# Two pairs of experts gathered at once from two fp32r parts, and each pair's second product behind the next pair's first ones

## The chip, the cores and the metric

The kernel runs on one core of one Trainium2 chip. The metric is the device time of one execution in microseconds (us); lower is better. The kernel before took 1582.65 us (median of 3 runs, 1581.34 to 1585.59). Engines are named as the profile names them: PE is TensorE's matmuls and PEld its weight loads, DVE is VectorE, ACT ScalarE, POOL GpSimd, SP SyncE, which issues most of the transfers from HBM.

## The reference

The program computes a two-layer first block over 256 tokens of 1024 features and then a two-layer second block. The change is in the first block alone, whose layers end with a mixture of experts:

```python
for i in range(DEPTH):                    # DEPTH = 2
    ...                                   # a token mixer and an attention over 256 memory tokens give o
    x = layer_norm(ALPHA * x + o, ln1_g[i], ln1_b[i])
    f = grouped_moe(x, router_w, router_b, w_gate[i], w_up[i], w_down[i])
    x = layer_norm(ALPHA * x + f, ln2_g[i], ln2_b[i])

def grouped_moe(x, ...):                  # 16 experts; each token goes to two of one group of four
    ...
    for e in range(N_EXPERTS):
        h = silu(xt @ w_gate[e]) * (xt @ w_up[e])        # 1024 -> 512
        out = out + combine[:, e:e + 1] * (h @ w_down[e])  # 512 -> 1024
```

All is fp32. `combine` is zero except for a token's two experts. setup_inputs draws the weights at random.

## The kernel before, in words

**Data.** The 256 tokens stand in two tiles of 128 (`TT = 2`), and the 1024 features in eight blocks of 128 (`KD = 8`). fp32 matmuls run in several passes of the array, so the larger products are written as sums of products of fp32r parts: `split` (L461 to L463) makes a high part with one ScalarE copy (L462) and the low part with one VectorE subtraction (L463). The expert products are fp32r too; the gather's are fp32.

**Experts.** An expert takes up to 64 tokens (`CAP = 64`), and the experts run in eight pairs, so that a pair fills the 128 positions of a tile: expert `ea` the first 64, `eb` the other 64. For a token that has the expert, `slot` holds its position there. Per pair `moe` (L1061 to L1193) does this:
- *gather* (L1076 to L1106): VectorE compares `slot` with a row of numbers (L1082), which gives a one-hot matrix `d` (tokens by positions); TensorE multiplies the standardised tokens `t` with it, sixteen fp32 matmuls of 128 columns (L1089), and `affine` evacuates the result with the norm's gain and bias into `xe` (features by positions). Then TensorE turns `d` (L1096) and fetches the combine weights of the positions (L1099).
- *up*: for two halves `j` of the features and for gate and up (`m`), four steps of 128 features, at each one matmul of `ea` (64 positions, 512 columns) and one of `eb` (L1139). The two write the two halves of one PSUM bank and use different columns of the array.
- ScalarE and VectorE compute the activation `eg` (L1148 to L1150).
- *scatter* of the pair before (L1113), then the gather of the next pair.
- four transposes of `eg` (L1159), evacuated by a ScalarE copy (L1160).
- *down*: for two halves of the output eight steps of 512 columns, `ea` and `eb` beside each other (L1169). ScalarE and VectorE evacuate each half in two fp32r parts, scaled by the combine weights (L1172, L1173); the next pair's scatter adds them to the tokens.

The first pair's gather is traced with a higher priority (offset 600), and its second half after the first half of pair 0's up matmuls. `scaled_rows` (L641) adds the tokens' own share in pair 0, with four row products on TensorE (L598). Behind the last scatter `keep_warm` (L592) issues matmuls whose results nobody uses.

**Before the experts.** `out_norm` (L884 to L923) ends the mixer with the product by `w_out`, then computes the moments, the router's chain of small VectorE operations (L942 to L1002), and the standardised tokens `t` (`standard`, L632). In layer 0 it also computes the other layer's memory products there (`mem_k`, `mem_v`); in layer 1 it issues 14 `keep_warm` matmuls.

**Loads.** Weights come in loads of 1 MiB, issued on SyncE's queue (L373) in a fixed order: gate, up and down are two loads each, so six for an expert and 96 for a layer. `Stream` puts a load into a slot of its own (eight) or, up to the number given by `limit`, into a slot lent from the first block's own `ESLOTS = 13`, which the mixer and `out_norm` use for their tensors. A slot becomes free when the matmuls that read it are done, and then the next load is issued. `out_norm` sets the limit to `ESLOTS - 5` in layer 0 and `ESLOTS - 2` in layer 1 and then to one more; `moe` to `ESLOTS - 2` and `ESLOTS - 1`, and from pair 6 on lower.

**Order.** A planner writes each engine's queue before the run. It takes what is ready by its own model of costs, by priority in the order in which the code traces the operations (`high_priority` moves them ahead). Matmuls that write the same PSUM bank stay in the order in which they are traced. On the chip an engine executes its queue in that fixed order, whatever is ready.

Of the kernel before, what the change touches and what calls it, by code (L numbers as in the profile page):

```python
# [17 lines left out]
P = 128  # L18
S = 256
TT = 2  # L20
D = 1024
KD = 8
NE = 16
CAP = 64
# [17 lines left out]
Q_UV = "gpsimd"  # L42
WARM0, WARM1, WARM2 = 12, 14, 22
E_X1 = "vector"
ESLOTS = 13
GCOL = 12
S0 = 0.0
S1 = 0.0
# [363 lines left out]
class Net:  # L412
# [240 lines left out]
    def first_block(self):  # L653
        nc, I, tc = self.nc, self.I, self.tc
        with ExitStack() as ctx:
# [15 lines left out]
            n = len(ROWS1)  # L671
# [44 lines left out]
            for i in range(2):  # L716
                if i:
                    xh, xl = sl.get([P, KD, S], F32R, "xh"), sl.get([P, KD, S], F32R, "xl")
                    tmp = sl.get([P, 4, 512], name="tmp")
                    self.scratch = itertools.cycle([tmp[:, k] for k in range(4)]).__next__  # L720
                    self.split_feat(t, KD, xh, xl, bias=self.ln_cols(0, "ln2"))
                    sl.put(tmp)
                parts = self.mixer(i, xh, xl, memT, t)
                route, t = self.out_norm(i, parts)
                t = self.moe(i, route, t)
                if self.stop in (f"x1_{i}", f"comb_{i}", f"x2_{i}"):
                    if self.stop == f"x2_{i}" and i:
                        self.scaled_rows(1, "ln2", t, self.xres, 1.0)
                        self.dumpit("x2_1", self.xres)
                    return None  # L730
# [60 lines left out]
    def mixer(self, i, xh, xl, memT, t2):  # L791
# [9 lines left out]
        if i == 0:  # L801
# [23 lines left out]
            chunk(0, lambda b, ps: nc.scalar.activation(uT[:, b], ps, AF.Gelu))  # L825
            sl.put(xh, xl)
            tok = sl.get([P, 2, 4, S], F32R, "tok")
            t = self.small([P, 512], "eg", bufs=1).rearrange("p (h t d) -> p h t d", h=2, t=TT)
            for hp in range(2):
                mix = self.psum("a").rearrange("p (h t d) -> p h t d", h=2, t=TT)  # L830
                for h in range(2):
# [54 lines left out]
    def out_norm(self, i, parts):  # L886


        nc, sl = self.nc, self.sl
        v = nc.vector  # L890
        x = self.xres
        st = [self.small([P, 2, 6], f"ln_st{tt}", bufs=1) for tt in range(TT)]
        raw = [self.psum("a")[:, :NE] for _ in range(TT)]
        self.stream.limit(ESLOTS - (2 if i else 5))
        for half in range(2):
            ps = [self.psum() for _ in range(TT)]
            run(self.gemm_stream(None, None, [("wout", i, half, j) for j in (1, 0)], ps,
                                 parts=[(p[:, 0], p[:, 1]) for p in parts]))
# [12 lines left out]
        sl.put(*parts)  # L911
        t = sl.get([P, TT, D], name="t")
        self.stream.limit(ESLOTS - (1 if i else 4))
        self.mom = self.moments(st, "ln")
        if i:
            self.keep_warm(WARM1, self.C("ident"), yT[:, 3])
        route = self.router(i, raw, self.mom)
        self.standard(x, t, self.mom)
        if i == 0:
            self.mem_k(1, "gpsimd")  # L920
            self.mem_v(1, "gpsimd")
            sl.put(self.mh, self.ml)
        return route, t  # L923

    def beats(self, s, name):

# [131 lines left out]
                for tt in range(TT):  # L1058
                    v.bn_stats(st[tt][:, half], f[:, tt, half * 512:half * 512 + 512])

    def moe(self, i, route, t):  # L1061


        nc, sl = self.nc, self.sl
# [1 line left out]
        comb, slot = route  # L1066
        f = self.xres
        self.dumpit(f"comb_{i}", comb)
        xe = self.small([P, KD, P], "xe", bufs=1)
        self.stream.limit(ESLOTS - (1 if i else 2))  # L1070
        iota = self.C("iota")
        cols = self.ln_cols(i, "ln1")

        def gather(pr):


            ea = 2 * pr
            d, sct = [x[:, 0].rearrange("p (t s) -> p t s", t=TT) for x in self.hl_pair(1, TT * P)]
            d = d.bitcast(F32).rearrange("p t (e c) -> p t e c", e=2)
            es = slice(ea, ea + 2)  # L1080
            for tt in range(TT):
                v.tensor_tensor(d[:, tt], iota[:, None, :].to_broadcast([P, 2, CAP]),  # L1082
                                slot[:, tt, es, None].to_broadcast([P, 2, CAP]), op=ALU.is_equal)
            for k4 in range(2):
                ps = self.psum("a").rearrange("p (k s) -> p k s", k=4)
                for k in range(4):
                    kk = 4 * k4 + k
                    for tt in range(TT):
                        nc.tensor.matmul(ps[:, k], t[:, tt, kk * P:kk * P + P],  # L1089
                                         d[:, tt].rearrange("p e c -> p (e c)"), start=tt == 0, stop=tt == TT - 1)  # L1090
                self.affine(xe[:, 4 * k4:4 * k4 + 4], ps, cols, 4 * k4, "va"[k4])
                if k4 == 0:
                    yield
            st = self.psum("a")
            for tt in range(TT):
                nc.tensor.transpose(st[:, tt * P:tt * P + P], d[:, tt].rearrange("p e c -> p (e c)"),  # L1096
                                    self.C("ident"))
            for tt in range(TT):
                nc.tensor.matmul(st[:, TT * P:TT * P + 2], d[:, tt].rearrange("p e c -> p (e c)"), comb[:, tt, es],  # L1099
                                 start=tt == 0, stop=tt == TT - 1)  # L1100
            v.tensor_copy(sct, st[:, :TT * P].rearrange("p (t s) -> p t s", t=TT))
            wt = self.small([P, 1], "slotw")
            for e in range(2):
                cs = slice(e * CAP, e * CAP + CAP)
                v.tensor_copy(wt[cs], st[cs, TT * P + e:TT * P + e + 1])
            yield sct, wt  # L1106

        def scatter(sct, y, half):
            hs = slice(half * 512, half * 512 + 512)
# [4 lines left out]
            for tt in range(TT):  # L1114
                v.tensor_tensor(f[:, tt, hs], f[:, tt, hs], ps[tt], op=ALU.add)

        last = None
        with self.tc.high_priority(offset=600):
            first = gather(0)
            next(first)  # L1120
        for pr in range(NE // 2):
            if pr == 6:
                self.stream.limit(0 if i else ESLOTS - 6)
                self.stream.keep = i
            ea, eb = 2 * pr, 2 * pr + 1
            if pr:
                sct, wt = nxt
            gu = [self.psum() for _ in range(2)]
            for j in range(2):
                if pr == 0 and j:  # L1130
                    sct, wt = next(first)
                for m in range(2):
                    w = [self.stream.get(("moe", i, e, 2 * m + j)).rearrange("p (k n) -> p k n", n=512)
                         for e in (ea, eb)]
                    for k in range(4):
                        kk = 4 * j + k
                        for e in range(2):
                            es = slice(e * CAP, e * CAP + CAP)
                            nc.tensor.matmul(gu[m][es], xe[:, kk, es], w[e][:, k], start=kk == 0,  # L1139
                                             stop=kk == KD - 1)  # L1140
                    for e in (ea, eb):
                        self.stream.done(("moe", i, e, 2 * m + j))
# [1 line left out]
                self.scaled_rows(i, "ln1", t, f, ALPHA)  # L1144
                self.dumpit(f"x1_{i}", f)
            g, u = gu
            eg = self.small([P, 512], "eg", bufs=1)
            nc.scalar.activation(eg, g, AF.Tanh, scale=0.5)  # L1148
            v.scalar_tensor_tensor(eg, eg, 1.0, g, op0=ALU.add, op1=ALU.mult)  # L1149
            v.scalar_tensor_tensor(eg, eg, 0.5, u, op0=ALU.mult, op1=ALU.mult)  # L1150
            if last is not None:
                for half in range(2):
                    scatter(last[0], last[1][half], half)
            if pr + 1 < NE // 2:
                *_, nxt = gather(pr + 1)
            hT = eg.rearrange("p (k s) -> p k s", k=4)
            pt = self.psum("a").rearrange("p (k s) -> p k s", k=4)
            for k in range(4):
                nc.tensor.transpose(pt[:, k], eg[:, k * P:k * P + P], self.C("ident"))  # L1159
            nc.scalar.copy(hT, pt)  # L1160
            last = sct, [self.hl_pair(1, 512) for _ in range(2)]
            for half in range(2):
                yh, yl = [x[:, 0] for x in last[1][half]]
                yp = self.psum()
                w = [self.stream.get(("moe", i, e, 4 + half)).rearrange("p (k n) -> p k n", n=512) for e in (ea, eb)]
                for k in range(4):
# [4 lines left out]
                    self.stream.done(("moe", i, e, 4 + half))  # L1171
                nc.scalar.activation(yh, yp, AF.Identity, scale=wt)  # L1172
                v.scalar_tensor_tensor(yl, yp, wt, yh.bitcast(F32), op0=ALU.mult, op1=ALU.subtract)  # L1173
        st = [self.small([P, 2, 6], f"ln_st{tt}", bufs=1) for tt in range(TT)]
        for half in range(2):
            scatter(last[0], last[1][half], half)
# [5 lines left out]
        else:  # L1182
            self.presplit([("w", 0, "fq", 0, "2")], lambda w, k: w[:, k:k + 1], 4)
        self.overflow(i, t, comb, slot, f, st)
        sl.put(t)
        self.mom = self.moments(st, "ln")
        if i:
            t = self.slots.get([P, TT, D], name="t2")
# [1088 lines left out]
```

## Time and profile before

| | |
|---|---|
| median of 3 runs | 1582.65 us |
| the profiled execution | 1589.67 us |
| its span, first to last instruction | 1588.0 us |
| mean granted TensorE clock | 0.98 |
| PE busy | 1489.8 us, 94% of the span |
| PEld busy | 1022.0 us |
| DVE busy | 897.8 us, 57% |
| ACT busy | 585.4 us, 37% |
| q1 (SyncE's transfers) | 335.61 MB |

All rows are of the one profiled execution, with times in us from the start of its span. Busy times are unions: two matmuls side by side count once. A row of a timeline groups like instructions that follow each other; its length runs from the first start to the last end, and matmuls overlap by a little over a tenth of a us, so the next row starts before the one above has ended. The granted clock is the share of full speed that the chip allowed TensorE. The expert stage of layer 0 lies from 141 to 385 us, that of layer 1 from 498 to 736 us.

### The profile page before, as it was taken

Reading aid. Unit: us, or ns where it says so; the run is one execution under the profiler, and the core shown is the slowest. Engines: PE = TensorE matmul, PEld = TensorE weight load, DVE = VectorE, ACT = ScalarE, POOL = GpSimd, SP = SyncE. Lnnn points to the kernel's source line nnn. Section 1 sums busy time; section 2 is a strip of 40 time slices with the busy share of each in tenths; the row PEclk is TensorE's granted clock in tenths of the full one; section 3 lists DMA queues with packets and bytes.
Section 4 is the critical chain, followed back from the end, with each engine's and each line's share of the span. In section 5 each row is a group of like instructions: output and inputs, shape, how many; then the busy total and the mean of one; then the engine's idle time right before and its main releaser. Section 6 shows DMA issues by size and latency. Waiting matters only on the chain.

```text
span 1588.0 us, 24343 instructions
## 1 busy us (share of the span) xinstructions
PE 1489.8 (94%) x9570; PEld 1022.0 (64%) x9570; DVE 897.8 (57%) x1906; ACT 585.4 (37%) x1196; POOL 83.2 (5%) x112
## 2 busy tenths in 40 slices
PE   9999999998999999998999889999999998899998
PEld 8885444433996445434766667777776676677776
DVE  6662323224775323224857778566766587784765
ACT  6541111111541111112645542355454565233653
POOL 0022000001000000003100010100000000010001
PEclk9999999999999999999999999999999999799999
DMA  9866999987284999964433442125454355211353
GB/s 362 342 245 244 398 421 421 421 345 319 81 316 184 395 421 421 421 252 166 139 106 118 148 146 68 55 93 186 159 201 150 113 174 179 69 64 41 117 202 133
DMA packets 56574, 350.75 MB, mean 221 GB/s; under 512 B 7434, under 2 KB 8456, under 8 KB 17030
## 3 DMA queue, kind: packets, MB, share of 16 engines
q1 hardware_dynamic: 51542, 335.61, 54.6%
q0 software_dynamic: 2112, 8.03, 1.5%
q10 hardware_dynamic: 2800, 5.49, 1.3%
q8 instruction: 77, 1.26, 0.3%
q14 instruction: 43, 0.35, 0.1%
HBM read 338.90 MB, written 3.67 MB: 216 GB/s over the span
## 4 chain that ended last, share of the span: by engine, by line
PE 39%; DVE 9%; DMA 2%; ACT 2%; issue 1%; ACTq 0%; DVEq 0%
PE ps_h L505 4%; PE ps_h L506 4%; PE ps_g L505 4%; PE ps_g L506 4%; PE ps_h L507 4%; PE ps_g L507 4%; PE ps_a L2022 3%; PE ps_b L2022 3%; PE ps_a L551 1%; DVE wl L463 1%; PE ps_a L1520 1%; DVE pad L2056 1%; PE ps_a L1543 1%; PE ps_b L551 1%; PE ps_b L1520 1%
## 5 line engine op out<-in xcount | busy, mean ns | idle before, releaser
L463 DVE TENSOR_TENSOR wl<-w_w,wh 128x512 fp32r<-128x512 f32 (+1 forms) x346 | 231.9, 685 | 116.4 <-ACT wh L462 115.3
L462 ACT ACTIVATE wh<-w_w 128x512 fp32r<-128x512 f32 (+1 forms) x354 | 215.4, 624 | 220.4 <-PE ps_g L507 90.0
L1139 PE MATMUL ps_g<-w_e,xe 128*64 128x512 f32 x616 | 184.8, 594 | 0.0
L506 PE MATMUL ps_h<-wl,hh 128*128 128x512 f32 (+2 forms) x272 | 109.3, 404 | 3.4 <-DVE wl L463 3.3
L506 PE MATMUL ps_g<-wl,hh 128*128 128x512 f32 (+2 forms) x272 | 109.0, 405 | 2.8 <-DVE wl L463 2.5
L1139 PE MATMUL ps_g<-w_x,xe 128*64 128x512 f32 x304 | 111.1, 594 | 0.0
L505 PE MATMUL ps_g<-wh,hh 128*128 128x512 f32 (+2 forms) x272 | 104.6, 409 | 4.5 <-ACT wh L462 4.1
L1139 PEld LDWEIGHTS ps_g<-w_e,xe 128*64 128x64 f32 x616 | 56.4, 137 | 80.9 <-issue 77.4
L507 PE MATMUL ps_h<-wh,hlo 128*128 128x512 f32 (+2 forms) x272 | 107.2, 396 | 0.0
L505 PE MATMUL ps_h<-wh,hh 128*128 128x512 f32 (+2 forms) x272 | 104.3, 404 | 2.9 <-ACT wh L462 2.1
L507 PE MATMUL ps_g<-wh,hlo 128*128 128x512 f32 (+2 forms) x272 | 105.7, 393 | 0.0
L1173 DVE SCALAR_TENSOR_TENSOR wl<-ps_g,slotw,wh 128x512 fp32r<-128x512 f32 x32 | 24.0, 751 | 126.6 <-ACT wh L1172 126.6
L1169 PE MATMUL ps_g<-w_e,eg 128*64 128x512 f32 x272 | 81.6, 596 | 6.8 <-ACT eg L1160 6.8
L1149 DVE SCALAR_TENSOR_TENSOR eg<-eg,ps_g 128x512 f32<-128x512 f32 x16 | 11.0, 688 | 119.7 <-ACT eg L1148 119.7
L462 ACT ACTIVATE wh<-w_x 128x512 fp32r<-128x512 f32 (+1 forms) x88 | 53.8, 623 | 57.0 <-PE ps_g L507 25.6
L1148 ACT ACTIVATE eg<-ps_g 128x512 f32<-128x512 f32 x16 | 9.6, 597 | 175.2 <-PE ps_g L1139 175.2
L583 ACT ACTIVATE xe<-ps_a,pcols 128x128 f32<-128x128 f32 x64 | 25.1, 457 | 121.2 <-PE ps_a L1089 117.0
L1089 PEld LDWEIGHTS ps_a<-wh,t_e 128*128 128x128 f32 x512 | 60.0, 192 | 12.0 <-issue 9.7
L506 PEld LDWEIGHTS ps_h<-wl,hh 128*128 128x128 f32 x272 | 51.9, 191 | 21.1 <-DVE wl L463 10.1
L1172 ACT ACTIVATE wh<-ps_g,slotw 128x512 fp32r<-128x512 f32 x32 | 22.0, 687 | 117.4 <-PE ps_g L1169 101.7
L1169 PE MATMUL ps_g<-w_x,eg 128*64 128x512 f32 x184 | 59.5, 596 | 5.7 <-ACT eg L1160 5.7
L506 PEld LDWEIGHTS ps_g<-wl,hh 128*128 128x128 f32 x272 | 52.3, 192 | 19.0 <-DVE wl L463 10.9
(783 smaller groups left out, 3212.9 us busy)
## 6 DMA issues: line engine op xcount, KB each, us to landing
w_e<-in_moe_dram SPq DMA_DIRECT2D x111, 1024.0 KB, 10.5
w_x<-in_moe_dram SPq DMA_DIRECT2D x61, 1024.0 KB, 10.6
w_w<-in_win_dram SPq DMA_DIRECT2D x56, 1024.0 KB, 4.9
w_w<-in_moe_dram SPq DMA_DIRECT2D x20, 1024.0 KB, 11.4
w_x<-in_wkv_dram SPq DMA_DIRECT2D x8, 1024.0 KB, 13.4
w_w<-in_wo_dram SPq DMA_DIRECT2D x8, 1024.0 KB, 4.9
w_x<-in_wout_dram SPq DMA_DIRECT2D x5, 1024.0 KB, 8.1
w_e<-in_winb_dram SPq DMA_DIRECT2D x5, 1024.0 KB, 9.6
```

The source lines that it names most:

```text
L462: self.nc.scalar.activation(hi, src, AF.Copy)
L463: self.q(eng).tensor_tensor(lo, src, hi.bitcast(F32), op=ALU.subtract)
L505: nc.tensor.matmul(o, xh[:, kk, ts], wh[:, k], start=f, stop=False)
L506: nc.tensor.matmul(o, xh[:, kk, ts], wl[:, k], start=False, stop=False)
L507: nc.tensor.matmul(o, xl[:, kk, ts], wh[:, k], start=False, stop=e)
L551: nc.tensor.transpose(ps[:rows, b, tt * P:tt * P + P], src[:, tt, (b0 + b) * rows:(b0 + b + 1) * rows], self.C("ident"))
L583: self.nc.scalar.activation(out[:, k], src[:, k], AF.Identity, bias=bk, scale=gk)
L1089: nc.tensor.matmul(ps[:, k], t[:, tt, kk * P:kk * P + P], d[:, tt].rearrange("p e c -> p (e c)"), start=tt == 0, stop=tt == TT - 1)
L1139: nc.tensor.matmul(gu[m][es], xe[:, kk, es], w[e][:, k], start=kk == 0, stop=kk == KD - 1)
L1169: nc.tensor.matmul(yp[es], hT[:, k, es], w[e][:, k], start=k == 0, stop=k == 3)
L1520: nc.tensor.matmul(s[:, h], qT[:, h0 + h, tt * P:tt * P + P], kT[:, h0 + h, :nk], start=True, stop=False)
L2022: ins = self.nc.tensor.matmul(out, lhsT, rhs, start=start, stop=stop)
```

## The change

- The standardised tokens `t` are split in `out_norm` into two fp32r parts, `th` and `tl`, by four ScalarE copies and four VectorE subtractions of 512 columns; they take two slots.
- `gather` serves two pairs at once: one-hot matrices of four experts (256 columns) are multiplied with both parts, four fp32r matmuls per block of features, 32 in all, and `xe` holds two pairs. Turning the one-hot matrix and fetching the weights follow for both pairs. The one-hot matrices lie in a slot of their own.
- A turn of the loop now traces: up of pair `pr`, the transposes of pair `pr - 1`, the scatter of pair `pr - 2`, in odd turns the gather of the pairs `pr + 1` and `pr + 2`, and down of pair `pr - 1`. A ninth turn has no up. The whole first gather stands ahead of up 0, at offset 600.
- `eg` has two buffers. `ESLOTS` is 12, so the limits of the loads change.

```diff
-ESLOTS = 13
+ESLOTS = 12
...
 out_norm:
-        self.stream.limit(ESLOTS - (2 if i else 5))
+        self.stream.limit(ESLOTS - (4 if i else 7))
...
         t = sl.get([P, TT, D], name="t")
-        self.stream.limit(ESLOTS - (1 if i else 4))
+        parts = [sl.get([P, TT, D], F32R, n) for n in ("th", "tl")]
...
         self.standard(x, t, self.mom)
+        for half in range(2):
+            hs = slice(half * 512, half * 512 + 512)
+            for tt in range(TT):
+                self.split(t[:, tt, hs], *(p[:, tt, hs] for p in parts))
...
 moe:
-        xe = self.small([P, KD, P], "xe", bufs=1)
-        self.stream.limit(ESLOTS - (1 if i else 2))
+        xe = self.small([P, KD, 2, P], "xe", bufs=1)
+        self.stream.limit(ESLOTS - (4 if i else 5))
...
+        oneslot = sl.get([P, 6, TT * P], F32R, "onehot")
...
 gather:
-            for k4 in range(2):
-                ps = self.psum("a").rearrange("p (k s) -> p k s", k=4)
-                for k in range(4):
-                    kk = 4 * k4 + k
-                    for tt in range(TT):
-                        nc.tensor.matmul(ps[:, k], t[:, tt, kk * P:kk * P + P],
-                                         d[:, tt].rearrange("p e c -> p (e c)"), start=tt == 0, stop=tt == TT - 1)
-                self.affine(xe[:, 4 * k4:4 * k4 + 4], ps, cols, 4 * k4, "va"[k4])
-                if k4 == 0:
-                    yield
+            for k2 in range(4):
+                ps = self.psum("a").rearrange("p (k s) -> p k s", k=2)
+                for k in range(2):
+                    kk = 2 * k2 + k
+                    for n, p in enumerate(parts):
+                        for tt in range(TT):
+                            nc.tensor.matmul(ps[:, k], p[:, tt, kk * P:kk * P + P],
+                                             d[:, tt].rearrange("p e c -> p (e c)"), start=n + tt == 0,
+                                             stop=n + tt == 2)
+                self.affine(xe[:, 2 * k2:2 * k2 + 2].rearrange("p k q s -> p k (q s)"), ps, cols, 2 * k2, "va")
...
+        for pr in range(pairs + 1):
+            if pr == 0:
+                with self.tc.high_priority(offset=600):
+                    slots[0], slots[1] = gather(0)
+            if pr == 6:
+                self.stream.limit(0 if i else ESLOTS - 7)
+                self.stream.keep = i
+            nxt = up(pr) if pr < pairs else None
+            if pr:
+                hT = turned(eg)
+                if last is not None:
+                    for half in range(2):
+                        scatter(last[0], last[1][half], half)
+                if pr % 2 and pr + 1 < pairs:
+                    slots[pr + 1], slots[pr + 2] = gather(pr + 1)
+                    if pr + 3 == pairs:
+                        sl.put(*parts)
+                sct, wt = slots.pop(pr - 1)
+                last = sct, down(pr - 1, hT, wt)
+            eg = nxt
```

`up`, `turned` and `down` hold the instructions that stood in the loop before, unchanged but for the doubled `xe`.

## Rows read from the trace of the kernel before

**Rows 1.** The page: busy share of DMA in 40 slices of 39.7 us.

```profile
DMA  9866999987284999964433442125454355211353
```

**Rows 2.** Windows: stretch, us, busy PE, PEld, DVE, ACT, POOL, clock, DMA, GB/s.

```profile
141.40:384.80 243.40, 231.96 (x1153) 102.27 (x1152) 64.83 (x135) 32.56 (x65) 0.00 (x0) 1.00 0.95 393
498.20:736.10 237.90, 227.84 (x1147) 101.42 (x1146) 65.15 (x138) 31.48 (x63) 0.00 (x0) 1.00 0.87 357
155.00:330.00 175.00, 167.46 (x861) 77.79 (x858) 49.37 (x106) 24.16 (x48) 0.00 (x0) 1.00 1.00 415
330.00:341.00 11.00, 11.00 (x58) 5.22 (x58) 2.28 (x7) 0.00 (x0) 0.00 (x0) 1.00 0.53 206
```

**Rows 3.** Timeline of TensorE, one pair of layer 0: start, length, operation [idle before].

```profile
172.23 0.59 PE L1139 MATMUL ps_g<-w_e,xe 128*64 128x512 f32 x1
...
186.06 0.73 PE L1113 MATMUL ps_a<-wh,wl 128*128 128x512 f32 x2
...
188.01 3.73 PE L1089 MATMUL ps_a<-wh,t_e 128*128 128x128 f32 x32
191.58 0.38 PE L1096 MATMUL ps_a<-consts,wh 128*128 128x128 f32 x2
...
192.17 0.63 PE L1159 MATMUL ps_a<-consts,eg 128*128 128x128 f32 x4
193.82 0.65 PE L1169 MATMUL ps_g<-w_e,eg 128*64 128x512 f32 x2 [1.02 <-ACT eg L1160]
...
200.74 0.60 PE L1139 MATMUL ps_g<-w_e,xe 128*64 128x512 f32 x2
```

**Rows 4.** Waits of TensorE, 141.4 to 384.9 us: total us, times, longest.

```profile
PE ps_g L1169 <- ACT eg L1160: 7.2, 8, 1.1
PE ps_a L1159 <- DVE eg L1150: 2.3, 3, 0.8
PE ps_a L1113 <- ACT wh L1172: 1.7, 2, 0.8
```

**Rows 5.** Groups by line, TensorE, 141.4 to 384.9 us: busy, mean ns, idle before.

```profile
L598 PE MATMUL ps_a<-rows,pick 50*128 50x512 f32 x4 | 1.5, 445 | 0.0
```

**Rows 6.** Timeline of TensorE, late pairs of layer 0.

```profile
286.19 1.46 PE L1169 MATMUL ps_g<-w_e,eg 128*64 128x512 f32 x6
287.48 1.02 PE L1139 MATMUL ps_g<-w_e,xe 128*64 128x512 f32 x2
288.43 0.74 PE L1113 MATMUL ps_a<-wh,wl 128*128 128x512 f32 x2
...
290.50 3.65 PE L1139 MATMUL ps_g<-w_e,xe 128*64 128x512 f32 x14
294.08 0.71 PE L1089 MATMUL ps_a<-wh,t_e 128*128 128x128 f32 x4
...
322.74 0.59 PE L1169 MATMUL ps_g<-w_x,eg 128*64 128x512 f32 x1
...
356.32 0.59 PE L1169 MATMUL ps_g<-w_e,eg 128*64 128x512 f32 x1
```

**Rows 7.** Timeline of SyncE's queue: the last expert loads of both layers.

```profile
341.37 0.90 SPq L373 DMA_DIRECT2D w_e<-in_moe_dram  x2
...
687.39 8.70 SPq L373 DMA_DIRECT2D w_x<-in_moe_dram  x4
```

**Rows 8.** DMA issues, 141 to 341 us: count, size, us from issue to landing.

```profile
w_e<-in_moe_dram SPq DMA_DIRECT2D x44, 1024.0 KB, 11.7
```

**Rows 9.** Timeline of TensorE in the mixer of layer 1.

```profile
404.47 0.28 PE L523 MATMUL ps_g<-xh_e,wh 128*128 128x256 f32 x1
404.59 0.28 PE L524 MATMUL ps_g<-xl_e,wh 128*128 128x256 f32 x1
```

**Rows 10.** Groups by line, weight loads, 404.7 to 413 us.

```profile
L523 PEld LDWEIGHTS ps_g<-xh_e,wh 128*128 128x128 f32 x24 | 4.6, 190 | 0.0
```

**Rows 11.** The page, costliest groups: busy, mean ns, idle before and its releaser.

```profile
L463 DVE TENSOR_TENSOR wl<-w_w,wh 128x512 fp32r<-128x512 f32 (+1 forms) x346 | 231.9, 685 | 116.4 <-ACT wh L462 115.3
```

More of the change, by code (lines that the diff above doesn't have):

```diff
@@ L723, in first_block @@
                 parts = self.mixer(i, xh, xl, memT, t)
-                route, t = self.out_norm(i, parts)
-                t = self.moe(i, route, t)
+                route, t, parts = self.out_norm(i, parts)
+                t = self.moe(i, route, t, parts)
                 if self.stop in (f"x1_{i}", f"comb_{i}", f"x2_{i}"):
@@ L827, in mixer @@
             tok = sl.get([P, 2, 4, S], F32R, "tok")
-            t = self.small([P, 512], "eg", bufs=1).rearrange("p (h t d) -> p h t d", h=2, t=TT)
+            t = self.small([P, 512], "eg", bufs=2).rearrange("p (h t d) -> p h t d", h=2, t=TT)
             for hp in range(2):
@@ L922, in out_norm @@
             sl.put(self.mh, self.ml)
-        return route, t
+        return route, t, parts
     def beats(self, s, name):
@@ L1059, in overflow, with moe @@
                     v.bn_stats(st[tt][:, half], f[:, tt, half * 512:half * 512 + 512])
-    def moe(self, i, route, t):
+    def moe(self, i, route, t, parts):
         nc, sl = self.nc, self.sl
@@ L1068, in moe @@
         self.dumpit(f"comb_{i}", comb)
-        xe = self.small([P, KD, P], "xe", bufs=1)
-        self.stream.limit(ESLOTS - (1 if i else 2))
+        xe = self.small([P, KD, 2, P], "xe", bufs=1)
+        self.stream.limit(ESLOTS - (4 if i else 5))
         iota = self.C("iota")
         cols = self.ln_cols(i, "ln1")
+        oneslot = sl.get([P, 6, TT * P], F32R, "onehot")
+        scts = [oneslot[:, n].rearrange("p (t s) -> p t s", t=TT) for n in range(4)]
+        onehot = oneslot[:, 4:].rearrange("p t (e c) -> p t e c", e=4)
@@ L1074, in gather @@
         def gather(pr):
             ea = 2 * pr
-            d, sct = [x[:, 0].rearrange("p (t s) -> p t s", t=TT) for x in self.hl_pair(1, TT * P)]
-            d = d.bitcast(F32).rearrange("p t (e c) -> p t e c", e=2)
-            es = slice(ea, ea + 2)
+            d = onehot
             for tt in range(TT):
-                v.tensor_tensor(d[:, tt], iota[:, None, :].to_broadcast([P, 2, CAP]),
-                                slot[:, tt, es, None].to_broadcast([P, 2, CAP]), op=ALU.is_equal)
@@ L1094, in gather @@
[L1094 to L1106, printed above, removed]
+                v.tensor_tensor(d[:, tt], iota[:, None, :].to_broadcast([P, 4, CAP]),
+                                slot[:, tt, ea:ea + 4, None].to_broadcast([P, 4, CAP]), op=ALU.is_equal)
+            for k2 in range(4):
[8 more added lines that the diff above has]
+                self.affine(xe[:, 2 * k2:2 * k2 + 2].rearrange("p k q s -> p k (q s)"), ps, cols, 2 * k2, "va")
@@ new lines, in gather @@
+            out = []
+            for q in range(2):
+                o = [d[:, tt, 2 * q:2 * q + 2].rearrange("p e c -> p (e c)").bitcast(F32) for tt in range(TT)]
+                st = self.psum("a")
+                for tt in range(TT):
+                    nc.tensor.transpose(st[:, tt * P:tt * P + P], o[tt], self.C("ident"))
+                for tt in range(TT):
+                    nc.tensor.matmul(st[:, TT * P:TT * P + 2], o[tt], comb[:, tt, ea + 2 * q:ea + 2 * q + 2],
+                                     start=tt == 0, stop=tt == TT - 1)
+                sct = scts[(pr + q) % 4]
+                v.tensor_copy(sct, st[:, :TT * P].rearrange("p (t s) -> p t s", t=TT))
+                wt = self.small([P, 1], "slotw", bufs=4)
+                for e in range(2):
+                    cs = slice(e * CAP, e * CAP + CAP)
+                    v.tensor_copy(wt[cs], st[cs, TT * P + e:TT * P + e + 1])
+                out.append((sct, wt))
@@ L1108, in scatter @@
+            return out
         def scatter(sct, y, half):
@@ L1115, in scatter, with up @@
                 v.tensor_tensor(f[:, tt, hs], f[:, tt, hs], ps[tt], op=ALU.add)
[L1117 to L1124, printed above, removed]
+        def up(pr):
             ea, eb = 2 * pr, 2 * pr + 1
-            if pr:
-                sct, wt = nxt
             gu = [self.psum() for _ in range(2)]
             for j in range(2):
-                if pr == 0 and j:
-                    sct, wt = next(first)
                 for m in range(2):
@@ L1138, in moe @@
                             es = slice(e * CAP, e * CAP + CAP)
-                            nc.tensor.matmul(gu[m][es], xe[:, kk, es], w[e][:, k], start=kk == 0,
+                            nc.tensor.matmul(gu[m][es], xe[:, kk, pr % 2, es], w[e][:, k], start=kk == 0,
                                              stop=kk == KD - 1)
@@ L1146, in moe @@
             g, u = gu
-            eg = self.small([P, 512], "eg", bufs=1)
+            eg = self.small([P, 512], "eg", bufs=2)
             nc.scalar.activation(eg, g, AF.Tanh, scale=0.5)
@@ L1150, in moe, with turned @@
             v.scalar_tensor_tensor(eg, eg, 0.5, u, op0=ALU.mult, op1=ALU.mult)
[L1151 to L1155, printed above, removed]
+            return eg
+        def turned(eg):
             hT = eg.rearrange("p (k s) -> p k s", k=4)
@@ L1160, in moe, with down @@
             nc.scalar.copy(hT, pt)
-            last = sct, [self.hl_pair(1, 512) for _ in range(2)]
+            return hT
+        def down(pr, hT, wt):
+            ea, eb = 2 * pr, 2 * pr + 1
+            y = [self.hl_pair(1, 512) for _ in range(2)]
             for half in range(2):
-                yh, yl = [x[:, 0] for x in last[1][half]]
+                yh, yl = [x[:, 0] for x in y[half]]
                 yp = self.psum()
@@ L1173, in moe @@
                 v.scalar_tensor_tensor(yl, yp, wt, yh.bitcast(F32), op0=ALU.mult, op1=ALU.subtract)
+            return y
+        pairs = NE // 2
+        slots, last, eg = {}, None, None
+        for pr in range(pairs + 1):
[18 more added lines that the diff above has]
+            eg = nxt
         st = [self.small([P, 2, 6], f"ln_st{tt}", bufs=1) for tt in range(TT)]
@@ L1184, in moe @@
         self.overflow(i, t, comb, slot, f, st)
-        sl.put(t)
+        sl.put(t, oneslot)
         self.mom = self.moments(st, "ln")
```

## The prediction

> **What bounds the kernel now.** I read the page's DMA slices first. The reader sees four slices at 9 in each of the two expert stages and mostly 5 or less behind them [rows 1]. So the question is what TensorE does in the two expert stages, the only ones that the diff changes much, and whether the loads leave it room.
>
> Next the windows by stage [rows 2]. From the first up matmul to the end of the last down matmul layer 0 takes 243.4 us and layer 1 237.9 us; TensorE is busy for 95% of both, at a granted clock of 1.00 (the upper of its two levels, 2.4 GHz). VectorE (64.8 us) and ScalarE (32.6 us) have room. DMA is saturated from 155 to 330 us at 415 GB/s, so a 1 MiB load takes 1.049 MB / 415 GB/s = 2.53 us and the twelve loads of a pair 30.3 us. That is longer than a pair takes on TensorE. TensorE stays ahead only because the stage starts with loads in store.
>
> Then one undisturbed pair in TensorE's timeline [rows 3]: up 172.23 to 186.06, 13.83 us; scatter of the pair before, 1.95; gather, 3.57; turning the one-hot matrix and fetching the slot weights, 0.59; four transposes, 0.63; a wait of 1.02 for ScalarE's copy of the transposed product; down, 6.92. Together 28.51 us. The waits view gives that wait once in each of the 8 pairs of a layer, 7.2 us [rows 4].
>
> Eight pairs by these rows (with 1.5 us of row products [rows 5], seven scatters and seven and a half gathers inside the window) make 226 us. The windows have 17.4 and 11.9 us more. Most of it is in the last pairs [rows 6]. There the queue is no longer in the regular order: one expert's first two matmul records (287.48), then scatter, then the other 14 records of that group (290.50). The order in the queue is written before the run by the planner, which puts other ready work where it expects the second expert's weights to be late. On the chip they aren't: the last load of layer 0 is issued by 342.3 us [rows 7], lands about 12 us later [rows 8], and is used in the last half of the last down product, from 384.8 - 3.5 = 381 us on. But the fixed order costs time, since two experts' matmuls share the array only when they stand next to each other. A split group takes 0.95 + 3.58 us, a whole one 13.83 / 4 = 3.46: 1.07 us lost. The ends of the down products (287.65 for pair 4, then 323.33, 356.91, and the window's 384.80) give pairs of 35.7, 33.6 and 27.9 us, where the regular ones would be 28.5, 28.5 and 24.35 (no gather in the last): 7.2, 5.1 and 3.5 too long.
>
> **The change part by part.**
>
> *Gather.* Removed: 16 fp32 records of 128 columns per half, 3.57 us per pair. Added: for two pairs 8 blocks x 2 parts x 2 token tiles = 32 fp32r matmuls of 256 columns. The trace has that form in the mixer: starts 0.12 us apart [rows 9], so 3.84 us for two pairs. Inside the window stood 7 x 3.57 + 1.9 = 26.9 us, and now 3 x 3.84 = 11.5: 15.4 us less per layer. The one-hot tails stay at 0.59 a pair. Evacuating into the doubled expert input is hidden: a down product of 6.92 us stands between a gather and the next up.
> The Trainium skill, "TensorE: Matmul & The Clock Gate", section on packing small matmuls, says that a weight load overlaps matmuls in flight only when it goes to other rows of the array. All loads of the gather go to all rows, so by it they would not be hidden. The trace disagrees: the same form has a load of 0.19 us for each matmul [rows 10] and still starts one every 0.12 us.
>
> *Wait before the second product.* A pair's transposes now stand behind the next pair's up, when its activation has long been done, and scatter (1.95) or gather stands between them and down, which covers the 1.02 us of the copy. 7.2 us less [rows 4]. Next in line is scatter's wait for the last y, 0.8 where it shows now [rows 4].
>
> *Start.* Up 0 now waits for the whole first gather and the tails of two pairs: 3.84 + 1.18 in place of the 1.9 (half of the 3.73 us record in [rows 3]) that stood there: +3.1 us. Before it the standardised tokens are split in two parts: four copies on ScalarE, idle there, and four subtractions on VectorE of 0.685 us [rows 11], 2.7 us, beside the router's chain of small operations on the same engine; 0 if they fit into its waits. In layer 1 TensorE has only filler matmuls (`keep_warm`) to do meanwhile: I take all 2.7. In layer 0 the other memory's products cover some: 0 to 2.7, I take 1.4. So +4.5 and +5.8 us.
>
> *Fewer loads in store.* The token parts and the one-hot buffers take three slots and the pool has one less, so four loads fewer are resident. They cost 4 x 2.53 = 10 us of lead on the chip and in the planner's reckoning. Bound on the chip, layer 0: last landing 342 + 12 + 10, less the 5 us that DMA idled at 330 to 341 [rows 2], plus the later start 4.5: 363.5; half a down product later 367. Layer 1: at 687.4 four loads were left [rows 7], with four more behind them 8 x 2.53 = 20 us: 707.5 + 5.8 + 3.5 = 717. Behind the stage the DMA slices of 3 to 4 hide the later prefetch.
>
> *Order written by the planner.* This I can't read. With four loads fewer and TensorE's queue 3 us shorter per pair, the planner will think the loads late sooner: now the first split is in the fifth pair of layer 0, a little later in layer 1. I take it from the fourth pair on, five pairs. Price of one: 3.5 as in the last pair, less 0.46, as the transposes' waits for the activation go, 2.3 us [rows 4] over five split pairs: 3.04; two of them carry a gather, at 2.7 more (the mean of 7.2 and 5.1, less 3.5). 5 x 3.04 + 2 x 2.7 = 21 us per layer. Ends: 0, and all eight pairs, 3 at 7.2 and 5 at 3.5: 39.
>
> *Sum.* Up and down 166.0, scatters 13.7, gathers 11.5, tails 6 x 0.59 = 3.5, transposes 5.0, row products 1.5, the end wait 0.8: 202 us. Layer 0: 202 + 21 + 4.5 = 227.5, saves 15.9; it would end at 368.9, just behind the loads' 367. Layer 1: 202 + 21 + 5.8 = 228.8, saves 9.1, ends at 727 where the loads allow 717. Together 25 us. The profiled execution took 1589.67 us (its span and 1.67 around it) and would take 1564.7; it is 7.0 above the median, which I correct by the same saving: 1582.65 - 25 = 1557.7.
>
> **The rivals.**
> 1. *The loads become the bound.* Without split groups TensorE would end at 348 and 706, but the loads allow 367 and 717: savings of 17.8 and 19, 37 us, 1546 us. For it: DMA at 415 GB/s with nothing to spare; fewer loads in store. Against: the planner already splits with more in store. 17%.
> 2. *Slower: split groups everywhere.* If the planner counts the loads late from the second pair on, 39 us of splits per layer give 202 + 39 + 4.5 = 245.5 and 246.8: 2.1 and 8.9 longer, 1594 us. It decides from some 34 us of splits per layer on. For it: a pair asks for its loads every 25 us now, with fewer in store. Against: seven scatters can't split more than a few groups each, and there are half as many gathers. 13%.
> 3. *The weight loads of the gather show.* 0.19 us for each of 4 x 32 matmuls, 24 us per layer: 1558 + 49 = 1607. The spacing of 0.12 speaks against it. It is the rule cited above. 1%.
> 4. *Even.* Splits of 30 to 36 us a layer eat the gain: 1578 to 1587. 11%.
> 5. *The wait stays.* The planner may put transposes and down together after all, since it issues what is ready: 16 x 1.02 = 16 us come back, 1574. Against: the next pair's up stands ahead by rank and its weights have long landed in the first half. 8%.
>
> **How the numbers follow.** My forecast has 50%, by itself 1546 to 1572 (split price 15 to 28 us a layer). A measurement here tells about 0.3%, 4.7 us, from no change. Faster: forecast, rivals 1 and 5, 75%. Within 0.3%: 11%. Slower: 14%. The range that holds 8 in 10 runs from 1544, just under the loads' bound, to 1586.
>
> **What would show it.** Right: the waits view loses the down product's wait for ScalarE; gather records 256 wide, 32 per two pairs, 0.12 apart; stages of about 228 us; the first up some 4.5 and 6 us later against the router's end; more split groups, first in the fourth pair. Wrong: waits of up or down for a load (rival 1), split groups from the second pair on (rival 2), transposes with a wait behind them (rival 5), or a loss outside of the expert stages, which I price at nothing.

## The result, and the profile after

The changed kernel takes 1564.5 us (median of 4 runs, 1563.3 to 1569.2), 0.988 of the kernel before, whose median beside it was 1584.1 (95% interval 0.986 to 0.991); in a second set of 5 rounds the ratio was 0.989 (0.986 to 0.992). It is 17 to 20 us faster: the forecast's side, inside its range, three quarters of its 25 us. Its profiled execution took 1564.14 us, its span 1562.5 against 1588.0.

The table is read from the timelines of TensorE: "start 1" runs from the first filler matmul ahead of layer 1's experts to the first up, a stage from the first up to the end of the last down, "behind" from there to the span's end.

| us | before | after | forecast for after |
|---|---|---|---|
| first up, layer 0 | 141.4 | 145.9 | 145.9 |
| stage 0 | 243.4 | 229.4 | 223.0 |
| between stage 0 and start 1 | 102.5 | 99.3 | 102.5 |
| start 1 | 10.8 | 17.0 | 16.6 |
| stage 1 | 237.9 | 228.0 | 223.0 |
| behind | 851.9 | 842.9 | 851.9 |

The windows of the changed kernel, with the columns of [rows 2]:

```profile
145.90:375.30 229.40, 216.00 (x997) 83.14 (x996) 60.71 (x111) 26.61 (x44) 0.00 (x0) 1.00 0.99 410
491.60:719.60 228.00, 215.41 (x997) 83.19 (x996) 60.65 (x111) 26.62 (x44) 0.00 (x0) 1.00 0.95 392
```

TensorE is busy 16 us less in layer 0 and 12 less in layer 1, and idle for 13 us in each, for 11 and 10 before. An early pair is as the forecast had it. TensorE's timeline of layer 0 from the transposes of pair 1 on:

```profile
201.05 0.66 PE L1157 MATMUL ps_a<-consts,eg 128*128 128x128 f32 x4
201.46 0.71 PE L1123 MATMUL ps_a<-wh,onehot_e 128*128 128x512 f32 x2
...
203.49 3.65 PE L1171 MATMUL ps_g<-w_e,eg 128*64 128x512 f32 x16
...
210.40 0.60 PE L1139 MATMUL ps_g<-w_e,xe 128*64 128x512 f32 x2
```

Transposes, scatter and down follow each other without an idle interval; the 1.02 us of [rows 3] is gone. With the up from 187.22 on the pair takes 23.2 us. The order breaks in the fourth pair, whose up starts at 210.40: its second group of 16 records is split into 2 and 14, with transposes, scatter and gather between:

```profile
213.94 0.55 PE L1157 MATMUL ps_a<-consts,eg 128*128 128x128 f32 x3
214.41 1.07 PE L1139 MATMUL ps_g<-w_e,xe 128*64 128x512 f32 x2
...
217.87 3.65 PE L1139 MATMUL ps_g<-w_e,xe 128*64 128x512 f32 x14
```

A late pair of the same layer, same view:

```profile
311.33 1.51 PE L1139 MATMUL ps_g<-w_x,xe 128*64 128x512 f32 x6
...
324.69 0.59 PE L1171 MATMUL ps_g<-w_e,eg 128*64 128x512 f32 x1
326.06 0.66 PE L1157 MATMUL ps_a<-consts,eg 128*128 128x128 f32 x4 [0.78 <-DVE eg L1150]
326.64 3.65 PE L1171 MATMUL ps_g<-w_e,eg 128*64 128x512 f32 x16
331.13 0.73 PE L1123 MATMUL ps_a<-wh,onehot_e 128*128 128x512 f32 x2 [0.83 <-ACT wh L1174]
...
337.05 0.73 PE L1123 MATMUL ps_a<-wh,onehot_e 128*128 128x512 f32 x2 [0.83 <-ACT wh L1174]
...
338.51 0.64 PE L1139 MATMUL ps_g<-w_e,xe 128*64 128x512 f32 x1
```

It takes 27.2 us. Every step stands right behind the one that feeds it: the transposes behind their own activation (0.78 us idle), each scatter behind the evacuation of its own down product (0.83, twice). Single up and down matmuls are mixed (324.69), so that some run without a partner. The waits of TensorE in stage 0 (total, times, longest) have one row left of [rows 4], and a larger one that was small there:

```profile
PE ps_a L1123 <- ACT wh L1174: 8.9, 11, 0.8
PE ps_a L1157 <- DVE eg L1150: 3.9, 5, 0.8
```

No matmul waits for a weight. One sentence ahead of the prediction is wrong: the expert products are fp32, two records for each matmul (an up of 32 matmuls has 64), not fp32r; only scatter, the four row products and now the gather are.

### The profile page after: what moved, and what is told of

It is laid out like the page before. It is cut to its first block, busy times and chain, and to the rows that moved or that the text cites. A ratio compares the mean times of both kernels' runs of the same rounds, so it can differ in the third digit from the quotient of the medians.

```text
span 1562.5 us, 23727 instructions
## 1 busy us (share of the span) xinstructions
PE 1460.5 (93%) x9314; PEld 983.6 (63%) x9314; DVE 893.8 (57%) x1866; ACT 584.1 (37%) x1172; POOL 83.0 (5%) x112
## 4 chain that ended last, share of the span: by engine, by line
PE 40%; DVE 8%; DMA 2%; ACT 2%; issue 1%; ACTq 0%; DVEq 0%
PE ps_h L506 4%; PE ps_g L506 4%; PE ps_h L505 4%; PE ps_g L505 4%; PE ps_g L507 4%; PE ps_h L507 4%; PE ps_a L2048 3%; PE ps_b L2048 3%; PE ps_a L551 1%; DVE wl L463 1%; PE ps_a L1546 1%; DVE pad L2082 1%; PE ps_b L1546 1%; PE ps_b L551 1%; PE ps_b L1569 1%
## 5 line engine op out<-in xcount | busy, mean ns | idle before, releaser
L463 DVE TENSOR_TENSOR wl<-w_w,wh 128x512 fp32r<-128x512 f32 (+1 forms) x338 | 228.4, 691 | 116.8 <-ACT wh L462 115.6
L1139 PE MATMUL ps_g<-w_x,xe 128*64 128x512 f32 x456 | 146.7, 595 | 0.0
L1139 PE MATMUL ps_g<-w_e,xe 128*64 128x512 f32 x440 | 145.1, 595 | 0.0
L1139 PEld LDWEIGHTS ps_g<-w_x,xe 128*64 128x64 f32 x456 | 44.6, 137 | 63.1 <-issue 61.9
L1139 PEld LDWEIGHTS ps_g<-w_e,xe 128*64 128x64 f32 x440 | 43.7, 137 | 57.4 <-issue 55.0
L1171 PE MATMUL ps_g<-w_e,eg 128*64 128x512 f32 x248 | 74.7, 597 | 0.0
L505 PEld LDWEIGHTS ps_h<-wh,hh 128*128 128x128 f32 x272 | 50.5, 190 | 19.3 <-ACT wh L462 9.1
L505 PEld LDWEIGHTS ps_g<-wh,hh 128*128 128x128 f32 x272 | 50.2, 189 | 19.0 <-ACT wh L462 9.8
```

The costliest lines, as they stand in the source:

```text
L463: self.q(eng).tensor_tensor(lo, src, hi.bitcast(F32), op=ALU.subtract)
L505: nc.tensor.matmul(o, xh[:, kk, ts], wh[:, k], start=f, stop=False)
L1139: nc.tensor.matmul(gu[m][es], xe[:, kk, pr % 2, es], w[e][:, k], start=kk == 0, stop=kk == KD - 1)
L1171: nc.tensor.matmul(yp[es], hT[:, k, es], w[e][:, k], start=k == 0, stop=k == 3)
```

## The experiments

P is the theory that the planner's order costs the time: from the fourth pair on it reckons with late loads and issues whatever is ready, as soon as it is. Ratios are to the kernel before in the same session, with 95% intervals.

**Tied order, on both kernels.** Each matmul and transpose of the expert loop is queued behind the one traced before it; this adds no wait on the chip.

```diff
+        def behind(op):
+            if queue:
+                self.tc.add_manual_dep(op.ins, queue[-1].name, ...)   # issue order only
+            queue.append(op.ins)
...
-                            nc.tensor.matmul(gu[m][es], ...)
+                            behind(nc.tensor.matmul(gu[m][es], ...))
```

> The changed kernel, with TensorE's instructions of the expert loop tied to the order in which the code traces them (issue order only, no waits added). Theory P (planner): from the fourth pair on the planner believes the loads late and puts each step right behind the one that feeds it, so that TensorE waits 0.8 us at each of them and runs matmuls of one expert alone; on the chip the weights are there. Then the regular order goes through all eight pairs, up to what the loads allow: the last expert load of layer 0 was issued at 345 us and takes 12, so the last down product ends at about 360 in place of 375, that of layer 1 at about 703 in place of 720, and the run takes 1530 to 1538 us. Theory L (loads): the late pairs are slow since their weights are late on the chip too; then the waits only move to the weights, the stages end within 3 us of where they did, and the run takes 1560 to 1569.

> The kernel before, with TensorE's expert loop tied to its traced order. Theory P: 226 us a stage in place of 243.4 and 237.9, so 17 + 12 = 29 us less, 1555 us, nearly ten us below the changed kernel without any of its edits. Theory L: within 0.3% of 1584.

The changed kernel with its order tied: 0.969 (0.966 to 0.972), 1535 us by that ratio. The kernel before: 0.984 (0.979 to 0.988), 1558. P holds for both, L for neither. The windows, first of the changed kernel tied, then of the kernel before tied:

```profile
145.40:359.00 213.60, 205.28 (x994) 86.72 (x994) 57.55 (x107) 26.49 (x44) 0.00 (x0) 1.00 0.99 409
478.00:688.00 210.00, 204.49 (x994) 86.90 (x993) 57.56 (x107) 26.47 (x44) 0.00 (x0) 1.00 0.99 411
```

```profile
140.00:366.10 226.10, 218.24 (x1150) 100.99 (x1149) 61.52 (x131) 31.70 (x65) 0.00 (x0) 1.00 1.00 413
484.40:710.40 226.00, 218.15 (x1149) 100.89 (x1149) 62.38 (x134) 31.06 (x63) 0.00 (x0) 1.00 0.91 371
```

226 us a stage is the prediction's sum of regular pairs for the kernel before. By the ratios tying the order gave it at least as much as the whole change did (0.984 and 0.988, with intervals that meet). The four stretches that the edits touch (up to the first up, the two stages, start 1) tell them apart: together they took 633.6 us in the kernel before, 604.0 with its order tied, and 620.3 in the changed kernel (before and changed 633.0 and 624.9 in the second profiles below). In the changed kernel, once tied, TensorE waits for weights, in stage 0:

```profile
PE ps_g L1147 <- DMA w_x<-in_moe_dram: 4.6, 4, 1.3
PE ps_g L1147 <- DMA w_e<-in_moe_dram: 2.8, 3, 1.3
PE ps_g L1147 <- DMA w_w<-in_moe_dram: 1.0, 1, 1.0
```

8.4 us, and 5.5 in stage 1, with DMA at 0.99. This is rival 1: it comes up only once the order is mended. The loads allow more than the prediction reckoned: the stages end 213.6 and 210.1 us behind their first up, where its 367 and 717 stood for 221 and 213.

**Each edit alone, order left to the planner.** Gather alone: the loop's turn is up, scatter, gather, transposes and down of the same pair. Order alone: the kernel before with the change's loop and its fp32 gather.

```diff
 gather alone:
-            nxt = up(pr) if pr < pairs else None
-            if pr:
-                hT = turned(eg)
+            eg = up(pr)
...
+            hT = turned(eg)
+            sct, wt = slots.pop(pr)
+            last = sct, down(pr, hT, wt)
```

> The changed kernel, but each pair's transposes and second product stand in its own turn again, as before the change: new gather, parts, slots and limits, old order. Theory P: regular work of 209 us a stage with the waits before the second product, five late pairs at 3.5 and two broken gathers at 2.7: 231.5 us, and starts 4.5 and 5.8 later: 8 us less than before, 1576. Rival A (the two edits add up as priced, with the order of the queue as before): the gather saves 15.4 less 4.5 and 5.8, 20 us, 1564.

> The kernel before with the change's order alone: the fp32 gather of one pair per turn as before, the second product behind the next pair's first ones; two slots fewer for loads, one-hot matrices in a slot of their own. Theory P: the 7.2 us of waits of a stage go in the regular pairs, and come back in the late ones, which cost 4.0 more each in this order than regular ones do: 1578 to 1588, no change. Rival A: 14 us less, 1570.

Gather alone 0.995 (0.991 to 0.998); order alone 0.999 (0.997 to 1.001). Both are P's numbers (stages of 234.0 and 233.1 us with the gather alone, for P's 231.5, and of 240.4 and 237.7 with the order alone). Order alone shows best where its gain went. Its waits in stage 0:

```profile
PE ps_a L1116 <- ACT wh L1169: 6.4, 8, 0.8
PE ps_a L1152 <- DVE eg L1145: 2.3, 3, 0.8
```

The 7.2 us before the second product are gone [rows 4], and scatter's wait for an evacuation has grown from 1.7 to 6.4.

**Each edit alone, order tied.**

> The kernel before with the change's order alone (fp32 gather), TensorE's order tied. If the prediction's term is right (7.2 us of waits a stage go, nothing else is moved), 14 us less than the kernel before with its order tied (0.9835 of before): 1544 us, stages of 219 us, ratio 0.975. If the waits only move: 1558.

> The changed kernel with the old order (transposes and second product in the pair's own turn), TensorE's order tied. By its own work a stage takes 209 us, 7 more than with the new order; the loads allow 213. If the loads are the bound, the new order has nothing left to give: 1535 to 1541 us, ratio 0.969 to 0.973, the waits for ScalarE's copy being there and the waits for weights that much shorter. If TensorE is the bound: 14 us more than with the new order, 1549, ratio 0.978.

Order alone, tied: 0.971 (0.969 to 0.974). Gather alone, tied: 0.971 (0.969 to 0.973). The windows, in this order:

```profile
140.90:358.10 217.20, 217.19 (x1149) 101.08 (x1149) 62.88 (x134) 31.73 (x63) 0.00 (x0) 1.00 0.99 409
474.10:691.40 217.30, 217.26 (x1149) 101.04 (x1149) 62.93 (x134) 31.72 (x63) 0.00 (x0) 1.00 0.97 396
```

```profile
146.80:360.80 214.00, 203.57 (x994) 85.19 (x994) 57.59 (x108) 26.67 (x44) 0.00 (x0) 1.00 0.99 409
483.00:693.20 210.20, 203.91 (x994) 84.76 (x993) 57.57 (x107) 26.64 (x44) 0.00 (x0) 0.99 0.99 411
```

Order alone has TensorE busy without a break: 226.1 - 217.2 = 8.9 us less a stage (217 for the 219 expected); the waits that went were 7.9 there. Gather alone ends its stages within 0.5 us of both edits together, although its waits before the second product are there:

```profile
PE ps_g L1179 <- ACT eg L1166: 5.4, 8, 0.7
PE ps_g L1147 <- DMA w_e<-in_moe_dram: 2.6, 2, 1.3
PE ps_g L1147 <- DMA w_x<-in_moe_dram: 1.5, 2, 1.3
```

They stand in the place of waits for weights, 4.1 us here against 8.4. So with the order tied the gather alone runs at what the loads allow, and the order alone at TensorE's own work, with no wait for a load. The four stretches together take 587.2 us with the order alone, 589.3 with the gather alone and 586.3 with both: the second edit adds next to nothing, and 0.969 against 0.971 is within the intervals.

**Fewer loads in store.** The limits alone are lowered, in the kernel before and in the changed kernel with its order tied.

```diff
 before, moe (the limits of out_norm and of pair 6 likewise):
...
-        self.stream.limit(ESLOTS - (1 if i else 2))
+        self.stream.limit(ESLOTS - (5 if i else 6))
...
```

> The kernel before with four expert loads fewer in store in both layers (the limits alone are lowered), as the change has. The prediction said that this costs 10 us of lead in the planner's reckoning, which then breaks up one more pair or two a layer: 4 to 15 us a layer, 1592 to 1614 in all. Theory P2: the planner's reckoning does not see the store, since there the loads are late from the first one on, and the order of TensorE's queue is what it was; on the chip the last load of layer 0 lands at 354 + 10 and is used from 381 on, so nothing waits: 1580 to 1588, no change.

> The changed kernel with TensorE's order tied (as in the first experiment), and four loads fewer in store. If the loads are the bound once the order is regular, every load of lead counts its 2.5 us: 10 us a layer later, 1535 + 20 = 1555 us, waits of up for its weights of about 18 and 15 us. If the bound is TensorE's own work: within 3 us of 1535.

The kernel before: 1.001 (0.998 to 1.004), no change. By SyncE's queue the edit took one load out of layer 0's store at the start (18 for 19) and none out of layer 1's, but delayed the rest: the last expert load was issued at 357 us for 342, and at 719 for 696. TensorE's order and its waits were those of [rows 4], the stages 243.3 and 237.9. So loads 15 and 23 us later cost this kernel nothing, and the planner's order did not answer to the limits. The changed kernel with its order tied went from 0.969 to 0.972 (0.969 to 0.975), not to 0.98: my 10 us a layer were wrong, as the edit did not take four loads. Counted from the first up, the last load was issued 3.5 and 3.3 us later, and the stages took 3.4 and 3.3 us more: there a late load counts in full.

**Half the loads.**

```diff
-                    w = [self.stream.get(("moe", i, e, 2 * m + j))... for e in (ea, eb)]
+                    w = [self.stream.get(("moe", i, e, 2 * m + j))... for e in (ea, ea)]
...
```

> The changed kernel with half the expert loads: the second expert of a pair uses the weights of the first, so 48 loads a layer in place of 96, and the second experts' outputs are not theirs; TensorE has the same instructions, and its order is left to the planner. Theory P: it is the loads in the planner's reckoning that break the order; with half of them its queue is regular through all eight pairs, and TensorE runs at its own pace: 202 us a stage (the prediction's sum of its work), 27 and 26 less, 1511 us. Rival B: the order is broken by something else that the planner reckons (PSUM banks, the pace of the other engines); then the stages keep most of 229 and 228 us, and the run takes 1545 to 1565.

0.955 (0.951 to 0.958), 1512 us by the ratio.

```profile
148.50:348.50 200.00, 200.00 (x994) 83.66 (x994) 57.58 (x107) 26.49 (x44) 0.00 (x0) 1.00 0.69 242
467.20:667.30 200.10, 200.10 (x994) 83.64 (x993) 57.62 (x107) 26.52 (x44) 0.00 (x0) 1.00 0.57 201
```

The planner, left alone, wrote the regular order through all eight pairs, and TensorE never idled. So the loads in its reckoning are what breaks the order, and 200 us is the stage's own work, where the prediction had summed 202. All that the broken order costs in layer 0 lies behind the start of the fourth pair's up: from there the stage takes 164.9 us in the changed kernel and 135.5 here.

**Both kernels again, for second profiles.**

> The changed kernel once more, for a second profile and a narrower ratio. In the first pair of profiles the two expert stages with their starts give 13 us, and stretches that the change does not touch give 12 more (3 between the stages, 9 behind the second), where the granted clock was 0.97 in the kernel before and 0.98 to 1.00 in the changed one. Theory R: these 12 are the runs' clock: the stages come out again within 1 us (229.4 and 228.0), the stretch behind the second stage anywhere between 843 and 852. Theory S: the change makes them shorter: 843 and 99 again, in this profile as in the first.

> The kernel before once more, for a second profile. Theory R: stages of 243.4 and 237.9 within 1 us, the stretch behind the second stage between 843 and 852, not tied to the kernel. Theory S: 852 and 102 again.

The numbers are theory S's: behind the stages 843.6 and 852.2 us, between stage 0 and start 1 99.3 and 101.1. Theory R allows them too, so two profiles of each kernel don't decide. The stages repeat to 0.1 us (229.4 and 228.0, 243.3 and 238.0). The windows behind them, changed kernel first:

```profile
724.20:1567.80 843.60, 783.26 (x5802) 599.44 (x5802) 595.87 (x1210) 401.62 (x837) 56.24 (x86) 0.98 0.38 128
```

```profile
734.10:1586.30 852.20, 786.72 (x5803) 601.86 (x5802) 597.33 (x1210) 400.94 (x837) 56.53 (x86) 0.98 0.37 127
```

The 8.6 us behind the stages are there again. Some 5 of them in the first run of the kernel before and 7 in the second lie in one stretch of the second block. Both runs lost granted clock there, at different places, and the first also waited 2.0 us for ScalarE. The first run, then the second:

```profile
1190.00:1200.00 10.00, 7.20 (x30) 4.78 (x29) 5.83 (x29) 3.73 (x7) 0.00 (x0) 0.93 0.36 114
1200.00:1222.00 22.00, 21.18 (x111) 16.76 (x110) 14.98 (x32) 10.95 (x19) 0.00 (x0) 0.95 0.41 153
```

```profile
1248.00:1262.00 14.00, 13.59 (x41) 10.51 (x42) 5.24 (x10) 4.36 (x9) 0.00 (x0) 0.52 0.30 94
```

The runs of the changed kernel show 0.86 at worst over 12 us there. In the nine single profiles of the other kernels the stretch behind the stages took 843 to 857 us, 852 in both with the gather alone and 849 in the changed kernel with its order tied and lower limits, so it doesn't follow the edits cleanly. What sets the clock there stays open.

## Why the prediction was right, and which step failed

*The work of a stage*: right. 202 us forecast, 200.0 measured with half the loads. The gather runs at the mixer's pace: 32 matmuls in 3.9 us at full clock. Each has its own weight load, of 0.19 us again:

```profile
L1096 PEld LDWEIGHTS ps_a<-onehot_e,th_e 128*128 128x128 f32 x48 | 7.5, 189 | 1.8 <-issue 1.6
```

So the loads are hidden, and rival 3 falls. The Trainium skill, "TensorE: Matmul & The Clock Gate", section on packing small matmuls, says in one bullet that a weight load overlaps running matmuls only in other rows of the array, and in the paragraph ahead of it also when it goes to a background weight buffer. These loads go to all rows, so the bullet, on which the prediction's rival went, does not hold for them.

*The start*: right in the first pair of profiles, +4.4 and +6.2 us for +4.5 and +5.8. In the second pair it was +8.3 (149.2 for 140.9) and +7.4 (18.3 for 10.8). Over all profiles the first up stands at 145.4 to 149.2 us with the new gather (seven profiles) and at 140.0 to 142.1 with the old one (six), and start 1 takes 17.0 to 18.3 and 10.8 to 13.2. That is about 6 us in each layer, so layer 0's term was some 1.5 us too small. Of layer 1's 6.2 some 2.0 are the subtractions in the router's chain, by TensorE's wait for its mask, in the changed kernel and in the kernel before:

```profile
483.21 0.38 PE L988 MATMUL ps_a<-mz,consts 128*128 128x32 f32 x2 [2.37 <-DVE mz L984]
493.99 0.38 PE L984 MATMUL ps_a<-mz,consts 128*128 128x32 f32 x2 [0.35 <-DVE mz L980]
```

The rest is the longer first gather, which ran there at a granted clock of 0.69, so in part at the lower of its two levels, 1.2 GHz. The two gathers, layer 1 and layer 0:

```profile
484.90:490.40 5.50, 5.46 (x33) 5.49 (x34) 2.03 (x6) 1.51 (x3) 0.00 (x0) 0.69 0.01 3
140.70:144.70 4.00, 3.98 (x33) 3.99 (x34) 1.93 (x4) 1.50 (x4) 0.00 (x0) 1.00 0.80 289
```

*The wait before the second product*: half right. It is gone, and rival 5 with it. But what is next in line was named wrongly: not 0.8 us at the very end but scatter's wait for an evacuation, eleven times, 8.9 us in stage 0.

*The order written by the planner*: this step failed in its size. The place was right (five pairs, from the fourth on), so rival 2 falls. The price was not 21 us but 229.4 - 200.0 = 29.4 and 27.9. The sum took the price of a late pair from the kernel before and let the transposes' waits go. The late pairs of the new order have more to lose: a late pair costs 27.2 - 23.2 = 4.0 us, three waits (2.4) and matmuls without a partner (1.6), against 3.04, and the transposes' waits rose from 2.3 to 3.9 us. That is 15 us more in two stages, less 4 by which the work was smaller than summed: why the stages with their starts gave 13 us, not 25 (8 in the second pair of profiles, for the longer starts). Rival 4's own figures are a little off: by the prediction's sum, splits of 30 to 36 us a layer come to 1576 to 1588 us, not 1578 to 1587.

*Fewer loads in store*: the count was right (SyncE's queue had issued 15 and 16 expert loads by the first up, in the kernel before 19 and 20), its part in the order not shown: lower limits made later loads and left the order as it was. An order that breaks a pair earlier would follow from the shorter pair alone, too; four loads fewer at the start, with the rest as before, were not tried. The first broken pair was the fifth and the sixth in the kernel before, the fifth in both layers with the order alone (17 and 18 loads), and the fourth with the gather alone (15 and 16): it moves with the loads, but the pairs get shorter along with them. Rival 1 did not occur, as its condition, no split groups, was not met.

*Outside of the stages*: priced at nothing, and 2 to 3 us between them and 9 behind were gained. Without these the total would have been about 1584 - 13 = 1571 us, or 1576 with the 8 us of the second pair. That it came as near as 1564.5 is in part their doing, and as no run shows their cause, in part luck.

## What to carry to other kernels

When an order is written ahead of the run, read TensorE's queue for steps that stand right behind their producer: there the planner believed the engine starved, and if the trace shows no wait for a transfer, tying the order is worth trying before any edit of the work. Here it gave 1.6% on the old kernel, where the change gave 1.2%, and 3.1% together with the change (0.969), the fastest version that loads all its weights. Measure an edit with the order tied as well; otherwise what it gives and what the planner makes of it come out as one number.

## What the hardware showed that was not expected

Single VectorE operations of the router's chain took 0.17 or 0.19 us in layer 1, and up to 1.31 us in layer 0, where GpSimd ran subtractions of about 1.3 us beside them. VectorE's timeline of the changed kernel in layer 0, and GpSimd's:

```profile
121.25 0.17 DVE L967 TENSOR_REDUCE gs<-tmp 128x8 f32<-128x32 f32 x1
121.46 0.82 DVE L974 TENSOR_TENSOR geq<-gs 128x32 f32<-128x32 f32 x1
122.20 1.31 DVE L975 TENSOR_TENSOR ggt<-gs 128x32 f32<-128x32 f32 x1
123.44 1.31 DVE L976 TENSOR_TENSOR geq<-geq,consts 128x32 f32<-128x32 f32 x1
124.78 0.19 DVE L977 TENSOR_TENSOR ggt<-ggt,geq 128x32 f32<-128x32 f32 x1
...
125.23 0.95 DVE L980 TENSOR_SCALAR gcnt<-gcnt 128x8 f32<-128x8 f32 x1
```

```profile
117.82 6.88 POOL L463 TENSOR_TENSOR wl<-w_x,wh 128x512 fp32r<-128x512 f32 x5 [6.86 <-ACT wh L462]
```

The slow operations with two inputs wait for GpSimd's end: the three from 121.46 on end 0.05 us behind subtractions that end at 122.23, 123.47 and 124.70. The one at 124.78 fell between two subtractions and took 0.19. The reduction at 121.25, with one input, does not wait. One input alone is no safeguard: the last row, a TENSOR_SCALAR, took 0.95 us beside the next subtraction, and 0.17 in layer 1. The Trainium skill, "SBUF — State Buffer", section on who interferes with whom, states this: a VectorE instruction with two inputs in SBUF contends with a GpSimd instruction that reads there, over a pair of ports that is an exclusive lock. The rows of the operations with two inputs agree.
